# Weight products in two parts: first and second part of a block in turns, instead of eight and eight

## The chip, the cores and the metric

One core of one Trainium2 chip runs the kernel. The metric is the device time of one execution in microseconds (us), as the median of several runs. Engines are named as in the profile: PE is TensorE's matmul, PEld its load of the stationary operand, DVE is VectorE, ACT ScalarE, POOL GpSimd, SP the engine that issues the loads of weights.

## The reference

One layer of a streaming encoder on 256 frames of width 2048, in float32. Two SwiGLU feed-forwards (width 5632) enclose a mixer of two head groups; each part works on an RMS-normalised input and adds to the residual.

```python
x = x + 0.5 * swiglu(rms_norm(x, ffn1_norm), w_gate, w_up, w_down)
p = rms_norm(x, mix_norm) @ w_in          # 2048 x 7456
y = concat(rwkv7_mix(p[..., :RWKV_COLS]), hgrn2_mix(p[..., RWKV_COLS:]))
x = x + y @ w_out
x = x + 0.5 * swiglu(rms_norm(x, ffn2_norm), ...)
return rms_norm(x, final_norm)
```

Nearly all of the arithmetic is in the products with the weights: three matrices of 2048 x 5632 in each feed-forward, `w_in` and `w_out` in the mixer. The mixer's recurrences (a generalised delta rule, and a gated linear recurrence in chunks) are small beside them.

## The kernel before, in words

**Products in parts.** A float32 matrix is split in two: hi is its value rounded to the type fp32r, lo is what is left. A product is hi x hi + hi x lo + lo x hi. With the weight block as the stationary operand (128 x 128), the activations of a slice k are stored as two halves side by side, hi and lo of 256 frames each. So hi of the weights meets 512 columns (both halves of the activations), and lo of the weights meets 256 columns (the first half alone). The function `columns` (L1171) issues the one or the other. Both add to the same accumulator tile `mm` in PSUM: `pt[:, n]` is a bank of 2 x 256 float32, one for each of two blocks n; the two halves of the bank are added when the job ends (`total`, L390).

**Jobs, pieces, units.** The work is a list of jobs (`job`, L387); a job makes 256 output columns from all slices k (16 in most jobs) and has its `consume` function called with the accumulator when the last product is issued. The weights of a job come in pieces of 512 KB: 128 x 1024 numbers, which are kp = 4 slices of 256 columns, so 8 blocks. (One job has kp = 8; two jobs, marked `tok`, have kp = 2 and take the activations as stationary operand and 512 columns of weights as moving one, first with hi of the weights for hi and lo of the activations, then with lo of the weights.) A unit is a slice of a piece with one part: `steps` (L1107) lists the four slices with part 0 and then the four with part 1. So TensorE does eight matmuls of 512 columns and then eight of 256. The first two pieces belong to two jobs and are done slice by slice; there, two matmuls with hi and two with lo follow each other (L1120).

**The main loop** (L1230) goes through the units. After each one it calls `tick` or `poll`: a tick moves the clock by which deferred work and the steps of the background tasks (the recurrences of the mixer, written as generators) are due; `poll` (L308) lets a due task make one step, if a model of the engines says that DVE and ACT are not too far behind. The ticks are counted in shares of a piece, two per piece. So matmuls of the background tasks stand between units in TensorE's queue. Each engine runs its own queue in order; the framework adds semaphores where data or buffers are shared.

**Weights on their way.** SP loads a piece to a `raw` tile (4 buffers, L195). `split` (L1142) then makes its two parts: an ACT cast gives hi, and a subtraction on DVE gives lo; where DVE is behind by the model, `spare` (L395) puts it on POOL. There are 4 buffers for hi and 4 for lo (`wsp`, L196). When the last unit of piece i has been issued, `split_to(i + 5)` (L1153) issues the split of piece i + 4 into the buffers of piece i, and the load of the piece four after that. The cast waits for the last matmul that reads hi of piece i, the subtraction for the cast and for the last one that reads lo.

**The end.** The last two jobs are not in the units: they do all products with lo first and then those with hi in two halves of the frames, so that the final norm of the first half overlaps the second (L1273 on).

Of the kernel before, what the change touches and what calls it, by code (L numbers as in the profile page):

```python
# [18 lines left out]
P = 128  # L19
# [156 lines left out]
def layer_kernel(ctx, tc, a, out):  # L176
# [4 lines left out]
    PE = Products(nc, model)  # L181
# [35 lines left out]
    def ps1():  # L217
        return psp.tile([P, 512], F32, tag="ps", name="ps")
# [89 lines left out]
    def poll():  # L308
        for task in bg[:2]:
            if task[1] <= clock[0] and max(V.until, S.until) <= model.now() + BEHIND:  # L310
                step(task)

    def tick():
        clock[0] += 1
        due = [x for x in later if x[0] <= clock[0]]
        for x in due:
            later.remove(x)
            x[1]()
        poll()


    class Norm:
# [51 lines left out]
        def operand(self, k):  # L374
            return self.parts[k // 2][:, k % 2]
# [729 lines left out]
        return [(jn, w[slab, chunks(chunk, i)], kp * i, kp) for i in range(nk // kp)]  # L1105

    def steps(i):  # L1107
        return [(i, kk, part) for part in range(2) for kk in range(pieces[i][3])]

    pieces, units = [], []  # L1110
    jn = 0
    while jn < len(jobs):
# [4 lines left out]
        else:  # L1117
            pieces += pieces_of(jn)
            jn += 1
    units = [(e, kk, part) for kk in range(4) for e in range(2) for part in range(2)]  # L1120
    for i, x in enumerate(pieces):
        if i >= 2 and x[0] < len(jobs) - 2:
            units += steps(i)
    raws, splits = {}, {}
# [28 lines left out]
    def split_to(n):  # L1153
        while state["split"] < min(n, len(pieces)):
            i = state["split"]
            load_to(i + 4)
            split(i, slice(0, pieces[i][3]))
            del raws[i]
            state["split"] += 1
# [11 lines left out]
    def columns(pt, w, x, n, part, start, stop):  # L1171
        w = w[:, n * P:(n + 1) * P]
        if part == 0:
            PE.matmul(pt.rearrange("p a t -> p (a t)"), w, x.rearrange("p a t -> p (a t)"), start=start, stop=stop)
        else:
            PE.matmul(pt[:, 0, :], w, x[:, 0, :], start=start, stop=stop)
# [50 lines left out]
    defer(15, n1[0].finish)  # L1227
    pts = {}
    ticks = 0
    for i, kk, part in units:  # L1230
        jn, _, k0, kp = pieces[i]
        _, _, _, nk, operand, consume, before, _, tok = jobs[jn]
        k = k0 + kk
        if k == 0 and part == 0:
            if before is not None:
                before()
            pts[jn] = mmp.tile([P, 2, 2, T], F32, tag="mm", name="mm")
        pt = pts[jn]
        x = operand(k)
        w = splits[i][part][:, kk, :]  # L1240
        start, stop = k == 0 and part == 0, k == nk - 1 and part == 1
        if tok:
            for b in range(2):
                o = pt[:, b].rearrange("p a t -> p (a t)")
                for e in range(2 - part):
                    PE.matmul(o, x[:, e, b * P:(b + 1) * P], w, start=start and e == 0, stop=stop)
        else:
            for n in range(1024 // kp // P):
                columns(pt[:, n], w, x, n, part, start, stop)
        if stop:  # L1250
            consume(pt)
            del pts[jn]
        ticks += (4 - 2 * part) / 3 / kp
        if ticks > 0.999:
            ticks -= 1
            tick()
        else:
            poll()
        if kk == kp - 1 and part == 1:
            splits.pop(i)  # L1260
            with tc.high_priority():
                split_to(i + 5)
# [3 lines left out]
    operand, nk = jobs[-1][4], jobs[-1][3]  # L1266
    ws = [[splits[i] for i in sorted(splits) if pieces[i][0] == jn] for jn in (len(jobs) - 2, len(jobs) - 1)]
# [5 lines left out]
    for h in range(2):  # L1273
        pt = mmp.tile([P, 4, T], F32, tag="mm", name="mm")[:, 0:2, :]
        for n in range(2):
            for k in range(nk):
                PE.matmul(pt[:, n, :], weights(2 * h + n, k, 1), operand(k)[:, 0, :],
                          start=k == 0 and n == 0, stop=k == nk - 1 and n == 1)
        x = xT_box[0][:, 12 + 2 * h:14 + 2 * h, :]
# [4 lines left out]
    for b in range(2):  # L1284
        for n in range(4):
            pt = ps1()[:, 0:2 * P].rearrange("p (a t) -> p a t", a=2)
# [62 lines left out]
```

## Time and profile before

| what | value |
|---|---|
| median of 3 runs | 2073.27 us (2073.06 to 2073.94) |
| the profiled execution | 2075.09 us |
| its span, first to last instruction | 2073.3 us |
| granted TensorE clock, mean | 0.994 |
| busy: PE, PEld, DVE, ACT, POOL | 98%, 86%, 67%, 49%, 18% |
| read from HBM | 362.24 MB, 177 GB/s over the span |

The busy time of PE is not its load: matmuls are pipelined, one begins before the end of the one ahead has been modelled, so the start times in the timeline say how fast they follow each other. Nearly all instructions are issued in two helpers (L148 for DVE, ACT and POOL, L168 for TensorE), so groups are told apart by the names of their tiles: `mm<-t,hi` is a product with the first part of the weights, `mm<-t,lo` one with the second.

### The profile page before, as it was taken

How to read it: one execution, taken by the hardware profiler on the slowest of the kernel's cores; microseconds unless marked ns; L12 is line 12 of the kernel's file. 1: busy time of each engine (PE TensorE's matmuls, PEld its weight loads, DVE VectorE, ACT ScalarE, POOL GpSimd, SP SyncE). 2: the span in 40 equal slices, each digit the busy share in tenths (PEclk: the TensorE clock that was granted, in tenths of full speed). 3: DMA queues.
4: the chain of work that ended last, by engine and by line, in shares of the span. 5: the costliest groups of instructions: out<-in, count | busy, mean ns of one | idle time of the engine just before them, and what ended most of it. 6: DMA issues, size and time to landing. Idle time of an engine off the chain costs nothing.

```text
span 2073.3 us, 30664 instructions
## 1 busy us (share of the span) xinstructions
PE 2034.2 (98%) x12286; PEld 1777.3 (86%) x12286; DVE 1384.4 (67%) x1502; ACT 1009.2 (49%) x1185; POOL 367.7 (18%) x218
## 2 busy tenths in 40 slices
PE   8999999999999999899989899999999999999997
PEld 7888888888888888788878788888888888888887
DVE  7655565565566687986898668856555655555557
ACT  6444443444344466455556545544444344434434
POOL 1211110110011122422343114211111011101101
PEclk9999999999999999999999999999999999999999
DMA  7555555555555565443334425555555555555553
GB/s 259 199 189 187 191 186 192 185 191 185 191 188 188 184 230 170 148 140 118 129 113 149 143 96 200 188 188 186 191 192 185 192 186 190 188 188 189 187 192 113
DMA packets 105983, 368.45 MB, mean 178 GB/s; under 512 B 11536, under 2 KB 17808, under 8 KB 105584
## 3 DMA queue, kind: packets, MB, share of 16 engines
q1 hardware_dynamic: 104352, 359.97, 51.9%
q0 software_dynamic: 944, 6.23, 0.8%
q8 instruction: 97, 1.59, 0.3%
q14 instruction: 46, 0.38, 0.1%
q10 hardware_dynamic: 544, 0.28, 0.0%
HBM read 362.24 MB, written 4.19 MB: 177 GB/s over the span
## 4 chain that ended last, share of the span: by engine, by line
PE 90%; DVE 5%; POOL 1%; issue 1%; ACT 1%; DVEq 0%; POOLq 0%; ACTq 0%
PE mm L168 85%; PE ps L168 5%; DVE t L148 3%; DVE lo L148 2%; POOL t L148 1%; ACT t L148 0%; POOL lo L148 0%; DVE xts L148 0%; PE ps L172 0%; DVE b L148 0%; POOL b L148 0%; DVE qk L148 0%; ACT hi L148 0%; ACT q L148 0%; DVEq L1345 0%
## 5 line engine op out<-in xcount | busy, mean ns | idle before, releaser
L168 PE MATMUL mm<-t,hi 128*128 128x512 f32 x5264 | 1329.5, 393 | 3.5 <-DVE t L148 3.1
L148 ACT CAST hi<-raw 128x1024 fp32r<-128x1024 f32 (+1 forms) x685 | 710.9, 1040 | 878.7 <-PE mm L168 764.5
L168 PEld LDWEIGHTS mm<-t,hi 128*128 128x128 f32 x5264 | 946.5, 189 | 174.3 <-ACT hi L148 3.6
L148 DVE TENSOR_TENSOR lo<-raw,hi 128x1024 fp32r<-128x1024 f32 (+1 forms) x613 | 773.5, 1264 | 447.1 <-ACT hi L148 427.6
L168 PEld LDWEIGHTS mm<-t,lo 128*128 128x128 f32 x5296 | 723.4, 190 | 65.8 <-POOL lo L148 7.9
L168 PE MATMUL mm<-t,lo 128*128 128x256 f32 x5296 | 745.1, 283 | 10.3 <-POOL lo L148 6.9
L148 POOL TENSOR_TENSOR lo<-raw,hi 128x1024 fp32r<-128x1024 f32 x72 | 176.1, 2446 | 555.2 <-ACT hi L148 518.0
L148 POOL TENSOR_TENSOR t<-t,inv 128x1024 f32<-128x1024 f32 x22 | 53.0, 2409 | 777.5 <-ACT t L148 777.5
L148 DVE TENSOR_TENSOR t<-t,t 128x512 fp32r<-128x512 f32 (+25 forms) x243 | 169.9, 702 | 11.3 <-ACT t L148 5.3
L148 DVE TENSOR_TENSOR t<-mm,t 128x512 f32<-128x512 f32 x122 | 83.3, 682 | 90.0 <-ACT t L148 89.9
L148 DVE SCALAR_TENSOR_TENSOR xts<-mm,xts 128x512 f32<-128x512 f32 x126 | 86.6, 688 | 76.1 <-PE mm L168 75.7
L148 ACT COPY t<-mm 128x512 f32<-128x512 f32 x122 | 71.0, 582 | 23.9 <-DVE t L148 20.6
L148 ACT CAST t<-t 128x512 fp32r<-128x512 f32 x72 | 44.1, 622 | 28.2 <-DVE t L148 24.8
L148 DVE TENSOR_TENSOR t<-t,inv 128x1024 f32<-128x1024 f32 (+1 forms) x35 | 46.3, 1322 | 1.0
L148 DVE RECIPROCAL t<-t 128x256 f32<-128x256 f32 x24 | 41.5, 1738 | 2.9 <-ACT t L148 2.9
L148 ACT ACTIVATE t<-t 128x1024 f32<-128x1024 f32 (+2 forms) x32 | 32.9, 1028 | 13.8 <-DVE t L148 13.6
L168 PE MATMUL ps<-q,t 128*128 128x128 f32 (+5 forms) x272 | 28.0, 260 | 7.0 <-DVE t L148 6.1
L148 DVE SCALAR_TENSOR_TENSOR t<-xts,vec,t 128x256 fp32r<-128x256 f32 x48 | 25.7, 558 | 13.3 <-ACT t L148 13.3
L168 PEld LDWEIGHTS ps<-q,t 128*128 128x128 f32 (+2 forms) x272 | 26.4, 174 | 9.3 <-issue 6.4
L148 ACT ACTIVATE t<-xts,vec 128x256 fp32r<-128x256 f32 x48 | 23.0, 505 | 22.5 <-DVE xts L148 20.4
L148 DVE SCALAR_TENSOR_TENSOR t<-t,vec,t 128x256 f32<-128x256 f32 x43 | 29.0, 720 | 6.3 <-POOL b L148 4.3
L148 POOL TENSOR_TENSOR t<-t 128x1020 f32<-128x1020 f32 (+1 forms) x7 | 17.8, 2549 | 84.1 <-DVE t L148 78.9
(134 smaller groups left out, 769.0 us busy)
## 6 DMA issues: line engine op xcount, KB each, us to landing
raw<-in_ffn_w_up_dram SPq DMA_DIRECT2D x176, 512.0 KB, 4.2
raw<-in_ffn_w_down_dram SPq DMA_DIRECT2D x176, 512.0 KB, 3.2
raw<-in_ffn_w_gate_dram SPq DMA_DIRECT2D x173, 512.0 KB, 3.4
raw<-in_w_in_dram SPq DMA_DIRECT2D x96, 512.0 KB, 3.2
raw<-in_w_out_dram SPq DMA_DIRECT2D x32, 512.0 KB, 3.2
raw<-in_w_i_dram SPq DMA_DIRECT2D x16, 512.0 KB, 3.3
raw<-in_w_lora_dram SPq DMA_DIRECT2D x6, 512.0 KB, 3.2
spill<-xts POOLq DMA_DIRECT2D x1, 2048.0 KB, 10.1
```

Of the source, the lines that this page charges most:

```text
L148: return fn(*args, **kwargs)
L168: return self.engine.matmul(out, a, b, **kwargs)
```

## The change

For each slice k and each block n the matmul with hi is now followed at once by the one with lo. A unit holds both parts; the loop over parts moves inside the loop over blocks. The first two pieces change in the same way, and in the `tok` jobs the two parts follow each other for each half of the frames. The tick is counted per slice (2 / kp, so after the second and the fourth slice of a piece of four), and `poll` or `tick` is called once for a slice instead of once for a slice and part. `columns`, the splits, the loads, the buffers and the last two jobs stay as they are.

```diff
     def steps(i):
-        return [(i, kk, part) for part in range(2) for kk in range(pieces[i][3])]
+        return [(i, kk, (0, 1)) for kk in range(pieces[i][3])]
...
-    units = [(e, kk, part) for kk in range(4) for e in range(2) for part in range(2)]
+    units = [(e, kk, (0, 1)) for kk in range(4) for e in range(2)]
...
-    for i, kk, part in units:
+    for i, kk, both in units:
...
-        if k == 0 and part == 0:
+        if k == 0:
...
-        w = splits[i][part][:, kk, :]
-        start, stop = k == 0 and part == 0, k == nk - 1 and part == 1
+        ws = [splits[i][part][:, kk, :] for part in both]
         if tok:
             for b in range(2):
                 o = pt[:, b].rearrange("p a t -> p (a t)")
-                for e in range(2 - part):
-                    PE.matmul(o, x[:, e, b * P:(b + 1) * P], w, start=start and e == 0, stop=stop)
+                for part in both:
+                    for e in range(2 - part):
+                        PE.matmul(o, x[:, e, b * P:(b + 1) * P], ws[part], start=k == 0 and part == 0 and e == 0,
+                                  stop=k == nk - 1 and part == 1)
         else:
             for n in range(1024 // kp // P):
-                columns(pt[:, n], w, x, n, part, start, stop)
-        if stop:
+                for part in both:
+                    columns(pt[:, n], ws[part], x, n, part, k == 0 and part == 0, k == nk - 1 and part == 1)
+        if k == nk - 1:
             consume(pt)
             del pts[jn]
-        ticks += (4 - 2 * part) / 3 / kp
+        ticks += 2 / kp
...
-        if kk == kp - 1 and part == 1:
+        if kk == kp - 1:
             splits.pop(i)
```

## Rows read from the trace of the kernel before

**Rows 1.** The page: PE's busy time, granted clock by slices, the chain by line

```profile
PE 2034.2 (98%) x12286; PEld 1777.3 (86%) x12286; DVE 1384.4 (67%) x1502; ACT 1009.2 (49%) x1185; POOL 367.7 (18%) x218
...
PEclk9999999999999999999999999999999999999999
...
PE mm L168 85%; PE ps L168 5%; DVE t L148 3%; DVE lo L148 2%; POOL t L148 1%; ACT t L148 0%; POOL lo L148 0%; DVE xts L148 0%; PE ps L172 0%; DVE b L148 0%; POOL b L148 0%; DVE qk L148 0%; ACT hi L148 0%; ACT q L148 0%; DVEq L1345 0%
```

**Rows 2.** The page's groups: busy us, mean ns of one, idle before, what ended it

```profile
L168 PE MATMUL mm<-t,hi 128*128 128x512 f32 x5264 | 1329.5, 393 | 3.5 <-DVE t L148 3.1
L148 ACT CAST hi<-raw 128x1024 fp32r<-128x1024 f32 (+1 forms) x685 | 710.9, 1040 | 878.7 <-PE mm L168 764.5
...
L168 PE MATMUL mm<-t,lo 128*128 128x256 f32 x5296 | 745.1, 283 | 10.3 <-POOL lo L148 6.9
```

**Rows 3.** Timeline of PE, 700 to 720 us: start us, us, what, count

```profile
702.06 2.00 PE L168 MATMUL mm<-t,hi 128*128 128x512 f32 x8
703.90 1.12 PE L168 MATMUL mm<-t,lo 128*128 128x256 f32 x8
704.85 2.00 PE L168 MATMUL mm<-t,hi 128*128 128x512 f32 x8
...
718.82 1.55 PE L168 MATMUL mm<-t,hi 128*128 128x512 f32 x6
```

**Rows 4.** Timeline of PE in a `tok` job: two pieces, 12 matmuls of 512 columns each

```profile
903.83 1.98 PE L168 MATMUL mm<-hi,t 128*128 128x512 f32 x8
...
906.55 1.98 PE L168 MATMUL mm<-hi,t 128*128 128x512 f32 x8
```

**Rows 5.** Timeline of PE in the last two jobs: 24 matmuls of 256 columns

```profile
2047.08 3.04 PE L168 MATMUL mm<-t,lo 128*128 128x256 f32 x24
2049.95 1.00 PE L168 MATMUL ps<-t,hi 128*128 128x256 f32 x7
```

**Rows 6.** Timeline of PE in the first two pieces: two and two in turns

```profile
8.27 0.63 PE L168 MATMUL mm<-t,hi 128*128 128x512 f32 x2
8.73 0.40 PE L168 MATMUL mm<-t,lo 128*128 128x256 f32 x2
8.97 0.65 PE L168 MATMUL mm<-t,hi 128*128 128x512 f32 x2
...
11.11 0.63 PE L168 MATMUL mm<-t,hi 128*128 128x512 f32 x2
```

**Rows 7.** Timeline of PE in the mixer: a single 512-column product among products with lo

```profile
1250.05 0.51 PE L168 MATMUL mm<-t,lo 128*128 128x256 f32 x3
1250.40 0.40 PE L168 MATMUL ps<-t,bones_r 128*128 128x512 f32 x1
1250.63 0.40 PE L168 MATMUL mm<-t,lo 128*128 128x256 f32 x2
1250.87 0.38 PE L168 MATMUL ps<-t,t 128*128 128x256 f32 x1
```

**Rows 8.** Timeline of ACT and DVE: the split of a piece in the steady stretch

```profile
704.10 1.05 ACT L148 CAST hi<-raw 128x1024 fp32r<-128x1024 f32 x1 [1.74 <-PE mm L168]
...
705.66 1.22 DVE L148 TENSOR_TENSOR lo<-raw,hi 128x1024 fp32r<-128x1024 f32 x1
```

**Rows 9.** PE's waits for lo, 13 to 2040 us: us in total, times, longest

```profile
PE mm L168 <- POOL lo L148: 6.9, 2, 5.8
PE mm L168 <- DVE lo L148: 3.4, 4, 1.6
```

**Rows 10.** Timeline of PE where it waits for lo, in brackets the idle time before

```profile
24.91 1.22 PE L168 MATMUL mm<-t,lo 128*128 128x256 f32 x8 [0.33 <-DVE lo L148]
...
27.97 1.21 PE L168 MATMUL mm<-t,lo 128*128 128x256 f32 x8
...
857.19 1.21 PE L168 MATMUL mm<-t,lo 128*128 128x256 f32 x8 [1.09 <-POOL lo L148]
...
1071.61 2.08 PE L168 MATMUL mm<-t,lo 128*128 128x256 f32 x8 [5.84 <-POOL lo L148]
```

## The prediction

> **What bounds the kernel now.** I read the page first. TensorE is busy 98% of the span, its clock is granted at nine tenths or more in all 40 slices (the 2.4 GHz level), and the chain that ended last lies for 85% of the span on the products into `mm` [rows 1]. These are two groups of nearly equal count: 5264 matmuls of 512 columns with the first part of a weight block (hi) and 5296 of 256 columns with the second (lo); almost nothing was waited for in front of either [rows 2]. So the spacing of these matmuls is the kernel, and the busy times, whose ends are modelled, don't give it. The timeline does: from the start of one run of eight hi to the next is one piece of weights; 702.06 to 718.82 us holds six pieces, 2.793 us each, of which eight hi take 1.84 and eight lo 0.95 [rows 3]. Per pair of one hi and one lo that is 0.3492 us. DVE, ScalarE and the DMA engines are behind TensorE: the ScalarE cast that makes hi waits 764.5 us in all for TensorE to free its buffer [rows 2].
>
> **Part 1: the order of the matmuls.** Counts, columns and operands stay; eight hi and eight lo of a piece become hi, lo, hi, lo. Switches between the two lengths go from two in a piece to sixteen. The trace shows what the lengths cost alone: twelve matmuls of 512 columns in a row (a step with tokens as stationary side) take 906.55 − 903.83 = 2.72 us, 0.2267 each [rows 4]; 24 of 256 columns take 2049.95 − 2047.08 = 2.87 us, 0.1196 each [rows 5]. A pair without any toll for switching would be 0.3463 us, a piece 2.770; the 2.793 of now is 0.023 above it for two switches.
>
> Two places of the trace show shorter turns. At the start of the kernel two hi and two lo take turns: hi at 8.27, lo at 8.73, hi again at 8.97, so 0.70 us for two pairs, 0.350 each [rows 6]. In the mixer single 512-column products of another kind fall among lo: three lo from 1250.05 (0.117 each), one of 512 columns at 1250.40, then lo at 1250.63 and two of them to 1250.87 [rows 7]. The single long one took 0.23 and its neighbours 0.12 each: 0.35 for the pair.
>
> So the toll grows with the length of a run and not with the number of switches: 0.023 for a cycle of eight and eight, 0.70 − 2 × 0.3463 = 0.007 for two and two. I take 0.350 us per pair, from the nearest rows [rows 6, 7]; against 0.3492 that is 0.0008 × 5264 = **+4 us**. The times of a row have two decimals, so a single reading is good to about 0.005 per pair, and the bounds must come from elsewhere. Below: no toll, 0.3463, −0.0029 × 5264 = −15 us. Above: the whole stretch of two and two from 8.27 to its fifth round at 11.11 holds eight pairs in 2.84 us, 0.355 each with some waiting in it [rows 6]: +0.0058 × 5264 = +31 us.
>
> The Trainium skill (TensorE: Matmul & The Clock Gate, section LDWEIGHTS) puts the load of 128 stationary columns at 128 / 1.2 GHz, 107 ns, and its step-by-step section lets the next load run under the running matmul. By that a load fits under 512 columns and just about fills 256; the number of loads under short matmuls stays eight per piece, and the order would not matter beyond the toll: as an estimate, zero. The 0.1196 of the short runs [rows 5], above the load's 107 ns, does not contradict it; no run here shows a load by itself.
>
> Each hi and the lo after it now add into the same accumulator bank back to back, where neighbours alternated between two. That is free: the step with tokens as stationary side already does it at 0.2267 [rows 4], the last products at 0.1196 [rows 5].
>
> **Part 2: lo is needed earlier.** The first lo of a piece runs second instead of ninth, 0.23 us after the start of the piece instead of 1.84. In the steady stretch this is covered: lo is made by DVE some 5 us after the start of the piece four before it (lo from 705.66 to 706.88 [rows 8], in the piece that began at 702.06), and used 4 × 2.793 = 11.2 us after that start; six us remain. Without cover the price is what the late lo blocks: seven hi, 7 × 0.23 = 1.6 us more per episode, since after the wait nearly the whole piece remains where now only eight lo do. Where TensorE waits for lo already, the cover is gone: six waits, 2 for POOL and 4 for DVE, 10.3 us in all [rows 9]. They stand in three stretches: 24.91 and 27.97 at the start, around 857.19, and around 1071.61 in the mixer [rows 10]. Within a stretch the waits share their lateness (lo comes when DVE or POOL gets to it, whatever TensorE did before), so I price each stretch once: 3 × 1.6 = **+5 us**. Bounds: nothing, if the planner's other choices happen to clear them; six waits, 6 × 1.6 = +10 us.
>
> **Part 3: hi is freed later.** The cast of the piece four ahead starts 0.2 us after the eighth hi (703.90 to 704.10 [rows 3, 8]); now hi is in use until the fifteenth matmul of sixteen, seven lo or 0.84 us later. Behind the cast on ScalarE wait copies out of the accumulator and the work of norms and mixer; behind those, DVE. DVE's lo and the free raw buffer move by the same 0.84, and with them the next load, which lands about 3 us after its issue. All of it still ends about five us ahead of use. If that cover were gone it would be 0.84 us per piece; I take zero, and the range holds what it adds in the mixer.
>
> **Part 4: the planner's steps.** A piece still makes two ticks at half and at the end of its TensorE time. Between ticks the mixer's background work is polled four times a piece instead of eight, so a step can start up to 0.35 us later. It is covered by products of weights except where TensorE waits for the mixer; zero, inside the range.
>
> **Sum.** +4 + 5 = +9 us. The profiled execution took 2075.09 us for a span of 2073.3; the three timed runs have a median of 2073.27. Nine us on the median give **2082 us**, 0.4% slower.
>
> **Rivals.**
> *The toll for switching goes.* If it belongs to long runs (for instance because the load under every lo is now the hi's, and the one under every hi has twice the time), a pair takes 0.3463: −15 + 5 = −10, **2063 us**; 2058 if no wait for lo grows either. For it: the toll shrank from 0.023 to 0.007 per cycle between eight and two. Against it: per pair, 0.0028 and 0.0037, it did not shrink at all, and the single long matmul of [rows 7] shows no gain. This ends on the other side of zero.
> *Every switch pays.* If a single hi after a lo is slower than in [rows 7], 0.355 as in the whole start: 31 + 5, **2109 us**; with the full 0.023 of a present cycle on each pair, 0.369, it would be +104, near 2180. Against this stands the 0.70 of [rows 6]. The deciding point is 0.350 per pair: above it the turns cost more than I say.
> *Waits in the mixer take over.* Six us of waiting for POOL in one place [rows 10] show that a planner's bad choice costs as much as my whole sum; a different order of polls can make one or remove one, so **2088 us** with one more of these and 2076 with this one gone. For it: the order of the background steps changes. Against it: one such place in the whole trace.
>
> **How the numbers follow.** A measurement of this kernel tells a change of 0.2%, 4 us, from none. The forecast, pairs at about 0.350 and some us of waits, gets 0.47: its own range is 2070 to 2095, of which 0.32 lies above +4 us, 0.12 within and 0.03 below. The toll going gets 0.28: 0.22 faster and 0.06 eaten up by waits. Every switch paying gets 0.15, all slower. The mixer taking over gets 0.10: 0.05 slower, 0.02 within, 0.03 faster (on the lower rate). Faster 0.28, same 0.20, slower 0.52. The range goes from 2057, the lower rival with few waits, to 2110, the near end of the upper one; about 0.1 lies above it and 0.08 below.
>
> **What would show it.** In the profile after, a steady stretch with turns of single matmuls: six pieces in 16.8 us mean my rate, 16.6 the lower rival, over 17.0 the upper. The count of lo and hi matmuls must be unchanged. Waits of TensorE for lo at the start and in the mixer should be longer by about 1.6 us per stretch, and the cast should start about 0.2 us after the fifteenth matmul of a piece. The prediction is wrong if the steady pair is below 0.348 or above 0.353, or if waits for lo appear outside the three stretches.

## The result, and the profile after

The changed kernel takes 2110.08 us (median of six runs, 2101.41 to 2110.42), the kernel before, run beside it, 2073.93 us (six runs, 2073.06 to 2075.15): 1.0158 times as long, 95% interval 1.0148 to 1.0168. It is 36 us slower, four times the +9 of the forecast and a hair above the range's upper end of 2110. The profiled execution is one of 2110.42 us, with a span of 2108.4 and a mean granted clock of 0.989.

The page of the changed kernel, from its parts on engines, slices and groups:

```profile
PE 2048.5 (97%) x12286; PEld 1778.7 (84%) x12286; DVE 1396.2 (66%) x1505; ACT 1008.7 (48%) x1184; POOL 356.2 (17%) x215
...
PEclk9999999999999999999999898999999999999999
...
L168 PE MATMUL mm<-t,hi 128*128 128x512 f32 x5264 | 1860.9, 398 | 19.2 <-DVE t L148 14.8
L168 PE MATMUL mm<-t,lo 128*128 128x256 f32 x5296 | 1485.1, 281 | 10.6 <-POOL lo L148 8.9
```

Against [rows 1, 2]: the same counts, 12286 matmuls, 5264 and 5296. The wait in front of lo is what it was (10.6 us, 10.3 before). The wait in front of hi went from 3.5 to 19.2 us, and two slices past the middle have a clock below nine tenths. The busy times of the two groups (1860.9 and 1485.1, from 1329.5 and 745.1) say nothing: a matmul that stands alone is credited with its modelled tail, which a run of eight shows once.

To see where the time went I put the two timelines side by side and compared the start of the first matmul with hi of the same piece in both:

| stretch | pieces | change in us |
|---|---|---|
| start | to 8 | +0.8 |
| first feed-forward | 8 to 256 | −4.8 |
| its end and the start of the mixer | 256 to 272 | +4.1 |
| mixer | 272 to 400 | +22.2 |
| end of the mixer, start of the second feed-forward | 400 to 424 | +6.5 |
| second feed-forward and the last two jobs | 424 to the end | +8.3 |

The sum is 37.1 at the start of the last matmul; 2.0 less lie behind it in this execution, which leaves the 35.1 by which the span grew. Two things stand out. The feed-forwards, which do the same work, changed in opposite directions, and some 29 us lie around the mixer, where I had counted about 2.

**Two spacings.** The timeline of PE, first at 700 us, then at 1600 us (the columns as in [rows 3]):

```profile
699.62 0.39 PE L168 MATMUL mm<-t,hi 128*128 128x512 f32 x1
699.85 0.28 PE L168 MATMUL mm<-t,lo 128*128 128x256 f32 x1
...
705.86 0.39 PE L168 MATMUL mm<-t,hi 128*128 128x512 f32 x1
...
1600.04 0.40 PE L168 MATMUL mm<-t,hi 128*128 128x512 f32 x1
...
1600.39 0.40 PE L168 MATMUL mm<-t,hi 128*128 128x512 f32 x1
...
1600.76 0.40 PE L168 MATMUL mm<-t,hi 128*128 128x512 f32 x1
...
1601.10 0.40 PE L168 MATMUL mm<-t,hi 128*128 128x512 f32 x1
...
1606.40 0.40 PE L168 MATMUL mm<-t,hi 128*128 128x512 f32 x1
```

Each stretch holds 18 pairs, from 699.62 to 705.86 and from 1600.04 to 1606.40: 6.24 us, 0.3467 a pair, in the first feed-forward, and 6.36 us, 0.3533, in the second. Before it was 0.3492 in both feed-forwards, as in [rows 3]. In the second the pairs go in threes: from 1600.04 on they take 0.35, 0.37 and 0.34 us, and the same again behind that; those of the first are even. A stretch that has one of the two spacings keeps it, for hundreds of us, until TensorE next has to wait or other matmuls come between. I call them quick and slow. Over 248 and some 240 pieces of eight pairs they make the −4.8 and most of the +8.3 of the table.

**Waits.** PE's waits over the whole run (us in total, times, longest), the changed kernel:

```profile
PE ps L168 <- DVE t L148: 17.6, 6, 10.9
PE mm L168 <- DVE t L148: 14.8, 5, 10.4
PE mm L168 <- POOL lo L148: 8.9, 2, 5.5
PE mm L168 <- DVE xts L148: 4.2, 4, 1.9
PE mm L168 <- DVE lo L148: 1.6, 1, 1.6
```

and the kernel before:

```profile
PE ps L168 <- DVE t L148: 11.1, 6, 5.4
...
PE mm L168 <- DVE t L148: 3.1, 3, 1.2
```

All lines of this view add to 52.9 us after and 30.4 before. Two waits of over 10 us, both for the mixer's own work on DVE, carry most of the 22.5 between them. The timeline of the changed kernel around both, all engines, in brackets the idle time before:

```profile
1169.94 1.40 PE L168 MATMUL ps<-q,t 128*128 128x128 f32 x5 [10.89 <-DVE t L148]
...
1295.23 3.31 DVE L148 TENSOR_TENSOR t<-t,t 128x1024 f32<-128x1024 f32 x1
...
1300.04 2.34 POOL L148 TENSOR_TENSOR t<-t,t 128x1024 f32<-128x1024 f32 x1 [2.58 <-DVE t L148]
1302.41 1.28 DVE L148 TENSOR_TENSOR t<-t,ps 128x512 f32<-128x512 f32 x2 [2.45 <-POOL t L148]
1303.13 1.22 ACT L148 CAST t<-t 128x512 fp32r<-128x512 f32 x2 [8.09 <-DVE t L148]
1304.52 0.80 PE L168 MATMUL mm<-t,hi 128*128 128x512 f32 x1 [10.44 <-DVE t L148]
...
1305.33 0.63 PE L168 MATMUL mm<-t,hi 128*128 128x512 f32 x1
...
1305.97 0.63 PE L168 MATMUL mm<-t,hi 128*128 128x512 f32 x1
```

The second wait is new. At 1294.08 TensorE has done the products with the first half of the recurrences' output and needs the second half, which is still being normalised: DVE, POOL, DVE, ACT one after the other, until 1304.5. POOL's step of this chain begins 6 us after TensorE ran out of work. In the kernel before it is this line of POOL's timeline, 9 us ahead of the first product with the second half (1282.24), so nothing waits:

```profile
1272.94 2.39 POOL L148 TENSOR_TENSOR t<-t,t 128x1024 f32<-128x1024 f32 x1 [5.32 <-DVE t L148]
```

Behind the wait the matmuls start at the 1.2 GHz level: a pair from 1305.33 to 1305.97 takes 0.64 us, not 0.35. So a wait costs more than its length. It shows in one window of both kernels (us, busy us of PE, PEld, DVE, ACT, POOL, granted clock, DMA share, GB/s), first before, then after; the changed kernel is 12 to 29 us behind there, so the two do not hold quite the same pieces:

```profile
1250.00:1350.00 100.00, 100.00 (x571) 88.02 (x571) 83.93 (x89) 56.28 (x70) 34.47 (x14) 1.00 0.54 184
1250.00:1350.00 100.00, 84.29 (x499) 70.85 (x498) 74.45 (x77) 42.11 (x57) 31.27 (x13) 0.93 0.39 137
```

PE was never idle in it before and is idle for 15.7 us after, and the granted clock drops from 1.00 to 0.93. Of the 37.1 us, 22.5 are idle time and 3.5 the two spacings. Most of the 11 left over is the lower clock: in all stretches with a granted clock of 0.50 together, PE is busy for 11.2 us before and for 25.4 us after. About half of the 14.2 more is lost, by the 0.64 and 0.35 of a pair; that is an estimate of 7 us. The rest, about 4 us, I put down to the turns' spacing inside the mixer, which is not shown.

### The profile page after: what moved, and what is told of

Same layout as the page of the kernel before. It is cut to its first block, busy times and chain, and to the rows that moved or that the text cites. A ratio compares the mean times of both kernels' runs of the same rounds, so it can differ in the third digit from the quotient of the medians.

```text
span 2108.4 us, 30658 instructions
## 1 busy us (share of the span) xinstructions
PE 2048.5 (97%) x12286; PEld 1778.7 (84%) x12286; DVE 1396.2 (66%) x1505; ACT 1008.7 (48%) x1184; POOL 356.2 (17%) x215
## 5 line engine op out<-in xcount | busy, mean ns | idle before, releaser
L168 PE MATMUL mm<-t,hi 128*128 128x512 f32 x5264 | 1860.9, 398 | 19.2 <-DVE t L148 14.8
L168 PE MATMUL mm<-t,lo 128*128 128x256 f32 x5296 | 1485.1, 281 | 10.6 <-POOL lo L148 8.9
L168 PEld LDWEIGHTS mm<-t,hi 128*128 128x128 f32 x5264 | 991.7, 188 | 256.2 <-DVE t L148 13.7
L148 DVE TENSOR_TENSOR lo<-raw,hi 128x1024 fp32r<-128x1024 f32 (+1 forms) x616 | 782.0, 1271 | 505.2 <-ACT hi L148 504.7
L168 PEld LDWEIGHTS mm<-t,lo 128*128 128x128 f32 x5296 | 1003.2, 190 | 13.1 <-POOL lo L148 9.6
L148 POOL TENSOR_TENSOR lo<-raw,hi 128x1024 fp32r<-128x1024 f32 x69 | 170.9, 2477 | 562.0 <-ACT hi L148 529.6
L168 PE MATMUL ps<-q,t 128*128 128x128 f32 (+5 forms) x272 | 28.5, 266 | 13.5 <-DVE t L148 12.1
L168 PE MATMUL mm<-hi,t 128*128 128x512 f32 x128 | 40.2, 395 | 0.0
L148 ACT COPY t<-ps 32x512 f32<-32x512 f32 (+8 forms) x44 | 19.7, 447 | 37.3 <-PE ps L168 36.5
## 6 DMA issues: line engine op xcount, KB each, us to landing
spill<-xts POOLq DMA_DIRECT2D x1, 2048.0 KB, 10.4
```

Of the source, the lines that this page charges most:

```text
L148: return fn(*args, **kwargs)
L168: return self.engine.matmul(out, a, b, **kwargs)
```

## Experiments

The kernel before ran beside every group: 2074.82 us beside the first four (twelve runs), 2075.15 beside the next four (fourteen), 2075.58 and 2074.84 beside the last two groups (seven each). None of these kernels leaves out a part of the computation.

### Is it the polls? Eight polls a piece with turns, and four without

In the changed kernel the background of the mixer is offered a step four times a piece, not eight. One run gives the changed kernel its polls back:

```diff
                 for part in both:
                     columns(...)
+                if n == 0:
+                    poll()
...
```

(The `tok` jobs get the same poll after the first half of the frames.)

> The changed kernel with a poll of the background tasks after the first block of a slice too, so eight polls a piece as before the change; matmuls in turns as in the changed kernel. Between piece 272 and piece 400 (the mixer) the changed kernel lost 22 us to the one before, most of it in two waits of 10.9 and 10.4 us for the recurrences. Theory (polls): these come from the recurrences being polled half as often; they go, and the time is 2084 to 2092 us. Rival (late lo and hi): the mixer loses because the second part is needed earlier and the first is freed later; the time stays at 2104 to 2112 us.

Measured: 2091.0 us (2087.43 to 2092.76), ratio 1.0072 (1.0057 to 1.0087). It is 16 us above before, where the changed kernel is 36. The mixer (pieces 272 to 400) now adds about 9 us in place of 22, and the wait ahead of the second half of the output projection is gone.

The other takes half of the polls from the kernel before:

```diff
-        else:
+        elif kk == 1:
             poll()
```

> The kernel before, eight and eight, but with four polls and ticks a piece instead of eight; nothing else. Theory (polls): the mixer loses some 22 us without any change of the matmuls' order, 2088 to 2102 us, with waits of TensorE for the recurrences of about 10 us each; the feed-forwards are as before to within 1 us. Rival (late lo and hi): 2070 to 2078 us.

Measured: 2083.95 us (2082.48 to 2085.39), ratio 1.0041 (1.0026 to 1.0056): +9, less than I had expected of it. But the wait that belongs to few polls is there again. The timeline of PE in this run:

```profile
1288.70 3.78 PE L168 MATMUL mm<-t,hi 128*128 128x512 f32 x8 [4.57 <-DVE t L148]
1292.28 1.91 PE L168 MATMUL mm<-t,lo 128*128 128x256 f32 x8
```

Again it stands ahead of the second half of the output projection, and again the matmuls behind it run at the lower level: eight hi take 3.58 us, where [rows 3] have 1.84.

### Where does it lie? Turns in one part of the kernel alone

Turns in the feed-forwards' jobs only, the mixer's jobs as before:

```diff
+    mix0 = len(jobs)
     mixer(to_ffn2)
+    mix1 = len(jobs)
...
     def steps(i):
+        if mix0 <= pieces[i][0] < mix1:
+            return [(i, kk, (part,)) for part in range(2) for kk in range(pieces[i][3])]
...
```

> Turns in the two feed-forwards alone; the jobs of the mixer go eight and eight with eight polls a piece. The mixer should be as in the kernel before. What is left: start +1, first feed-forward -5 by its spacing, its end +4 (TensorE waits for DVE to empty the accumulator), second feed-forward +8 if its matmuls fall into the slow spacing of 0.3533 us a pair, -5 if into the quick one of 0.3467. Theory (the spacing is one of two, set where a stretch begins): about 2082 us or about 2069 us, and the spacing within a feed-forward is one of these two numbers and no other. Rival (the spacing belongs to the place: quick in the first, slow in the second): always 2082 us.

Measured: 2081.0 us (median of nine, 2079.72 to 2094.82), ratio 1.004 (1.0025 to 1.0055): +6. The first feed-forward is quick and the second slow, as in the changed kernel, so this run does not tell the theory from the rival. The run of 2094.82 us has no profile; it lies above the median by about what a slow first feed-forward would add (248 pieces of 0.053 us, 13 us), and its granted clock, 0.995, is no lower than that of the others.

Turns and their four polls in the mixer's jobs only (the condition above with `not`):

> The counterpart of the run with turns in the feed-forwards alone: turns with four polls a piece in the jobs of the mixer, eight and eight with eight polls in the feed-forwards. Theory (the mixer holds most of the loss, by its background steps, and the parts add): 2074 + 27 = 2101 us, 2095 to 2106, with the wait ahead of the second half of the output projection of about 10 us. Rival (the mixer loses because it is entered at another time and state from the feed-forward): 2070 to 2085 us.

Measured: 2102.25 us (2098.15 to 2103.72), ratio 1.0125 (1.0108 to 1.0142): +27, and not a tenth of a us of it in the steady stretches of the feed-forwards. Its waits of PE:

```profile
PE ps L168 <- DVE t L148: 17.6, 6, 10.9
PE mm L168 <- DVE t L148: 15.3, 5, 10.4
```

The longest, 10.9 and 10.4, are those of the changed kernel to the tenth. And 27 and 6 make 33 of the 36. So the two parts are nearly independent, and three quarters of the loss are the mixer's.

The fourth corner, turns in the mixer with eight polls (the poll after the first block put into the run above, for units that hold both parts):

> Turns in the mixer's jobs alone, as in the run with turns there, but with a poll after the first block of each slice, so eight polls a piece as before. The theory that the turns are nearly harmless in the mixer and that their 27 us come with the halved polls: the two waits of over 10 us at the head of the second half of the output projection and ahead of the products of the attention go, about +9 us remain as in the kernel that had turns everywhere and eight polls, so 2083 to 2087 us, ratio 1.004 to 1.006. The rival that the turns themselves put the mixer out of step, whatever the polls: 2096 us or more, with at least one of the two waits still near 10 us. A halved poll that costs the same with and without turns (9 us) would give 27 - 9 = +18, 2093 us.

Measured: 2086.46 us (2085.15 to 2089.91), ratio 1.0059 (1.0042 to 1.0076). Its waits:

```profile
PE ps L168 <- DVE t L148: 9.9, 4, 6.9
PE mm L168 <- DVE lo L148: 9.1, 4, 3.6
...
PE mm L168 <- DVE t L148: 1.7, 2, 1.1
```

The 10.4 us are gone, the 10.9 have become 6.9; in their place DVE's lo is late, up to 3.6 us. All waits add up to 31.6 us, only 1.2 more than before; where the rest of the +12 lies is shown further down. That gives a square of four: eight polls and the old order 0, four polls and the old order +9, eight polls and turns +12, four polls and turns +27. Halving the polls costs 9 us without the turns and 15 with them; the turns cost 12 with eight polls and 18 with four. Neither is harmless by itself, and together they cost 6 us more than their sum. The theory had the size of the run right, but it had called the turns nearly harmless, and 12 us are not that.

### Does an earlier need for lo do it? And do more polls help?

The old order with a piece's eight lo ahead of its eight hi:

```diff
     def steps(i):
-        return [(i, kk, part) for part in range(2) for kk in range(pieces[i][3])]
+        kp, first = pieces[i][3], not pieces[i][2]
+        return ([(i, 0, 0)] if first else []) + [(i, kk, 1) for kk in range(kp)] + [(i, kk, 0) for kk in range(first, kp)]
...
```

> The kernel before, eight and eight with eight polls, but with the eight lo of a piece ahead of the eight hi (the first slice of a job still begins with hi). So lo is needed at the start of a piece and hi freed at its end, as in the changed kernel, without single turns and without fewer polls. Theory (late hi at the ends of the stages): spacing 0.349 in both feed-forwards; the end of the first feed-forward loses 2 to 4 us and the end of the mixer 3 to 7, the start 1 to 2: 2079 to 2088 us. Rival (these losses belong to the turns or the polls): 2071 to 2077 us.

Measured: 2087.0 us (2084.58 to 2089.01), ratio 1.0059 (1.0042 to 1.0075): +12, of it about 6 in the mixer, 3 at its end, and one or so each at the start and at the end of the first feed-forward. That is inside the theory's range, but half of it lies in the mixer, where the theory had put nothing. PE waits 12.4 us for POOL's lo (6.9 before), 6.8 at the longest. So an order that needs lo early does cost in the mixer, but the two waits of the changed kernel are not in this run.

Sixteen polls a piece in the kernel before:

```diff
             for n in range(1024 // kp // P):
                 columns(pt[:, n], w, x, n, part, start, stop)
+                if n == 0:
+                    poll()
```

> The kernel before, eight and eight, with a poll after the first block of a unit too: sixteen polls a piece instead of eight. Theory (fewer polls are late polls, so more of them do no harm): 2066 to 2076 us. Rival (the mixer's order was fitted to its eight polls, and any other number spoils it): 2079 to 2090 us, as with four polls.

Measured: 2087.51 us (2086.26 to 2088.69), ratio 1.006 (1.0045 to 1.0075): +12. My theory in its plain form (few polls make steps late, more do no harm) falls here. No wait ahead of the second half of the output projection, but another one, and behind it again eight hi at the lower level (3.75 us, 2.00 in [rows 3]); the timeline of PE:

```profile
1087.69 3.75 PE L168 MATMUL mm<-t,hi 128*128 128x512 f32 x8 [9.34 <-DVE t L148]
```

Four different edits that move what the mixer is offered by fractions of a us (half the polls, twice the polls, lo first, turns with eight polls) each cost 9 to 12 us. Waits are only a part of that. The table has all waits of PE, and how long PE is busy in the stretches with a granted clock of 0.50, each from the profiled execution:

| kernel | median against before, us | PE's waits, us | PE busy at 0.50, us |
|---|---|---|---|
| before | 0 | 30.4 | 11.2 |
| four polls, old order | +9 | 32.8 | 22.8 |
| sixteen polls, old order | +12 | 37.7 | 20.3 |
| lo first | +12 | 36.0 | 17.0 |
| turns in the mixer, eight polls | +12 | 31.6 | 26.2 |
| turns in the mixer, four polls | +27 | 51.3 | 23.0 |
| the changed kernel | +36 | 52.9 | 25.4 |

Take half of what the last column has above its first row as time lost. Then added waits and clock together come within 4 us of each difference up to the +27. In the run with four polls in the old order, and in that with turns in the mixer and eight polls, the lower clock costs more than the added waits. One such stretch of the latter run, where PE had waited 1.98 us at 862.54 (columns as in the windows above):

```profile
863.94:870.76 6.82, 6.52 (x31) 5.43 (x31) 6.68 (x9) 0.58 (x1) 0.00 (x0) 0.50 0.68 244
```

What is special to few polls is one wait, that for the recurrences ahead of the output projection: 10.4 us, 10.4 and 4.6 in the three runs with four polls, none in those with eight or sixteen.

### What sets the two spacings?

In the profile after, stretches that begin with a hi after a wait for the accumulator are mostly slow, and those that begin with a lo mostly quick. So I suspected the first matmuls of a stretch. The run with turns in the feed-forwards only, with each feed-forward job's first slice as hi, hi, lo, lo, and turns from there:

```diff
+            if k == 0 and len(both) == 2:
+                for part in both:
+                    for n in range(2):
+                        columns(...)
...
```

> As the run with turns in the feed-forwards alone (2081.0 us), but the first slice of every job there goes hi, hi, lo, lo; after it hi, lo in turns. So the turns are broken once in every job, in both feed-forwards in the same way. Theory (the spacing of a stretch is set by what came ahead of it and kept till the next break): both feed-forwards show the same spacing in their steady parts, either 0.3467 us a pair (about 2068 us) or 0.3533 (about 2090 us). Rival (the spacing belongs to the place): quick in the first, slow in the second as before, 2079 to 2085 us.

Measured: 2080.86 us (2079.53 to 2084.9), ratio 1.003 (1.0019 to 1.004). The jobs do not share a spacing, they alternate. The timeline of PE in two neighbouring jobs:

```profile
103.06 0.40 PE L168 MATMUL mm<-t,hi 128*128 128x512 f32 x1
...
104.83 0.40 PE L168 MATMUL mm<-t,hi 128*128 128x512 f32 x1
...
115.05 0.40 PE L168 MATMUL mm<-t,hi 128*128 128x512 f32 x1
...
117.13 0.40 PE L168 MATMUL mm<-t,hi 128*128 128x512 f32 x1
```

Five pairs in 1.77 us, 0.354, and six in 2.08, 0.347; so it goes on through both feed-forwards, and the mean, 0.350, is about that of before. The same beginning turns slow to quick and quick to slow. That the beginning gives the spacing is refuted in my wording, and so is the rival that the place in the kernel does, since both feed-forwards do the same. What is left: a break in the turns can flip the spacing, and what stood ahead counts.

Next, in place of a change of order, something foreign ahead of the turns: two products of 128 x 1 numbers, in float32, of a tile of zeros into a scratch tile that nothing reads, written once ahead of piece 448. The profile shows each as two matmuls.

```diff
+        if i == 448 and kk == 0:
+            kick = ps1()
+            for b in range(2):
+                PE.matmul(kick[:, b:b + 1], sts[0][:, 0, :], ones[:, 0:1], start=True, stop=True)
```

> As the run with turns in the feed-forwards alone, with two tiny float32 products (128 x 1, zeros) ahead of piece 448, once, in the second feed-forward after its last wait. In the changed kernel's trace such products stood ahead of two stretches (764.7 and 886.5 us), and both were quick. Theory (set by what came ahead): from there to the end the second feed-forward is quick, 0.3467 instead of 0.3533 a pair over 226 pieces of 8 pairs, 12 us less: 2066 to 2071 us. Rival (the place): 2079 to 2085 us, and nothing changes at piece 448.

Measured: 2068.44 us (median of six, 2067.9 to 2080.62), ratio 0.9979 (0.9961 to 0.9998), 12.6 below the same kernel without them. In the profiled execution they ran earlier than written, at 1343.77: nothing holds them, and they fell where, without them, a load of TensorE waits 0.43 us for DVE. Behind them the stretch is quick, to the end; without them it turns slow at that place and stays so. One of the six runs took 2080.62, about the time of a slow first feed-forward more, at a granted clock of 0.995, no lower than the others'; that run has no profile.

Then the test that takes the mixer out of it: turns only in the steady pieces of both feed-forwards (16 to 239, and 448 to the end), the rest as before, with the tiny products ahead of each stretch and without:

```diff
     def steps(i):
+        if not (16 <= i < 240 or i >= 448):
+            return [(i, kk, (part,)) for part in range(2) for kk in range(pieces[i][3])]
...
+        if i in (16, 448) and kk == 0 and 0 in both:
+            kick = ps1()
+            for b in range(2):
+                PE.matmul(kick[:, b:b + 1], sts[0][:, 0, :], ones[:, 0:1], start=True, stop=True)
```

> Turns only where nothing waits: pieces 16 to 239 and 448 to the end, each begun with the two tiny products; all else eight and eight with eight polls, so start, ends of stages and mixer as in the kernel before. Theory: each piece in turns saves 0.0200 us (2.7933 - 8 x 0.3467), 224 + 226 pieces, 9 us: 2064 to 2067 us, faster than both kernels. Rival (the place): the first stretch saves 4.5 us, the second loses 7.5: 2076 to 2079 us.

Measured: 2066.03 us (2065.52 to 2069.04), ratio 0.9961 (0.9947 to 0.9975). It beats both kernels, by 9 and by 44 us. The same kernel without the second hunk:

> The run with steady turns (2066.0 us) without its two pairs of tiny products, so that the turns at pieces 16 and 448 begin straight behind eight lo. Theory (what stands ahead sets the spacing): in the run with turns in the feed-forwards alone the turns that began behind eight lo at 1320 us were slow; both stretches become slow, 0.3533 a pair, 450 pieces x 0.053 = 24 us more, about 2090 us; one of them slow, 2078 us. Rival (the tiny products do nothing and steady stretches are quick once nothing waits in them): 2064 to 2068 us.

Measured: 2089.04 us (2087.88 to 2091.12), ratio 1.0066 (1.0051 to 1.0081). The timelines of PE, with the products:

```profile
55.77 0.88 PE L168 MATMUL mm<-t,lo 128*128 128x256 f32 x6
56.49 0.50 PE L168 MATMUL ps<-cst,st 128*128 128x1 f32 x4
56.85 0.47 PE L168 MATMUL mm<-t,hi 128*128 128x512 f32 x1
...
400.14 0.39 PE L168 MATMUL mm<-t,hi 128*128 128x512 f32 x1
...
406.38 0.39 PE L168 MATMUL mm<-t,hi 128*128 128x512 f32 x1
```

and without:

```profile
400.04 0.40 PE L168 MATMUL mm<-t,hi 128*128 128x512 f32 x1
...
406.40 0.40 PE L168 MATMUL mm<-t,hi 128*128 128x512 f32 x1
```

Again 18 pairs each: 0.3467 with them, 0.3533 without, for the whole of both stretches. 450 pieces at 2.793 − 8 × 0.3467 = 0.020 us less make the 9 us; the other way it is 450 × 0.033 = 15 us, where 13.5 are measured. That what stands ahead of the turns decides which of the two spacings they take is shown; turns right behind eight lo are slow, turns behind the tiny products quick. What in TensorE holds the state is open. The trace does not tell the two apart but by the start times: in both a load begins with the matmul ahead of it.

## Why the prediction was right or wrong

The direction was right, slower at a chance of 0.52; the size was not. Step by step:

**What bounds the kernel.** Held. TensorE remains the bound, the counts are unchanged, and the steady stretches end on its spacing alone.

**Part 1, the rate.** The forecast took one rate for the whole kernel, 0.350, and +4 us. There are two, 0.3467 and 0.3533, so that both marks I had set for being wrong were met, below 0.348 and above 0.353. The first is the rival in which the toll goes (0.3463), the second close to the one in which every switch pays (0.355); I had set them against each other as alternatives, and the kernel does both. The net of both feed-forwards was −4.8 + 8.3 = +3.5, and the +4 agrees with it by chance only. The step that failed is reading a rate out of 0.70 us for two pairs [rows 6] or one single product [rows 7]: rows that short can't show that a rate has two values. The Trainium skill (TensorE: Matmul & The Clock Gate, section LDWEIGHTS) gives a load one duration by its columns, 107 ns for 128; from that no two spacings of one and the same sequence would follow, and the measurement decides.

**Part 2, lo needed earlier.** The forecast was 1.6 us in each of three stretches, +5. Of [rows 10] the line at 27.97 shows no wait: of the six waits of before one lies at the start, two around 850, three around 1070. The timeline of PE after, in the same three stretches, in the second and third at other pieces than before:

```profile
24.61 0.39 PE L168 MATMUL mm<-t,lo 128*128 128x256 f32 x1 [1.62 <-DVE lo L148]
...
840.57 0.58 PE L168 MATMUL mm<-t,lo 128*128 128x256 f32 x1 [3.42 <-POOL lo L148]
...
1083.06 0.58 PE L168 MATMUL mm<-t,lo 128*128 128x256 f32 x1 [5.52 <-POOL lo L148]
```

Each is now the only wait for lo of its stretch. The start has 1.3 us more, nearly as priced, though only 0.8 of it is left eight pieces into the kernel; the second stretch has 1.8 more, the third 2.9 less, so that the sum of waits for lo is 10.5 us against 10.3. The stretches were right, the sum of +5 isn't found in the waits for lo. With turns everywhere and eight polls it is: 12.4 us for DVE's lo and 2.8 for POOL's, 4.9 more than before. With turns and eight polls in the mixer alone the sum is 10.9. How late lo is depends on what else DVE and POOL have been given.

**Part 3, hi freed later: zero.** In the steady stretches it is zero, and the cast starts 0.2 us behind the fifteenth matmul of a piece, as forecast. At the end of the first feed-forward something is lost: the accumulator comes free late there. The timeline after:

```profile
742.82 2.39 POOL L148 TENSOR_TENSOR lo<-raw,hi 128x1024 fp32r<-128x1024 f32 x1 [2.92 <-ACT hi L148]
742.85 3.44 DVE L148 TENSOR_TENSOR lo<-raw,hi 128x1024 fp32r<-128x1024 f32 x1
...
746.55 1.41 DVE L148 SCALAR_TENSOR_TENSOR xts<-mm,xts 128x512 f32<-128x512 f32 x2
...
748.10 0.56 PE L168 MATMUL mm<-t,hi 128*128 128x512 f32 x1 [1.93 <-DVE xts L148]
```

TensorE waits 1.93 us for DVE to empty its accumulator, and DVE had a lo ahead of that in its queue, which took 3.44 us and not the 1.22 of [rows 8]. The kernel before has no wait there. The prediction said that copies out of the accumulator wait behind the cast, and then priced it at nothing. But the later hi alone does not make this wait. The run with turns in the feed-forwards and the tiny products (2068.44 us) does the same as the changed kernel up to there, and its lines at this place are:

```profile
741.46 1.22 DVE L148 TENSOR_TENSOR lo<-raw,hi 128x1024 fp32r<-128x1024 f32 x1
741.91 3.03 POOL L148 TENSOR_TENSOR lo<-raw,hi 128x1024 fp32r<-128x1024 f32 x1 [3.13 <-ACT hi L148]
```

Here DVE begins ahead of POOL, its lo takes 1.22 us, and TensorE waits 0.3. In the changed kernel POOL begins its lo 0.03 us ahead of DVE, and DVE's ends 1.08 us after POOL's. Of the 616 lo that DVE makes in that trace, the 547 with no POOL instruction beside them take at most 1.23 us, and 38 of the other 69 take longer. So what is lost here hangs on which of two subtractions begins first: pieces 256 to 272 add 4.1 us in the changed kernel, 0.4 in the run with the tiny products, and 0.3 with turns everywhere and eight polls.

**Part 4, half the polls: zero.** This is the step that failed most. The prediction wrote that a later step is covered "except where TensorE waits for the mixer", and then put zero for just that place. It is the place that mattered: turns and polls together cost 27 us there in a run by themselves. The polls alone cost 9, the turns alone 12, so the prediction's silence on what the turns do inside the mixer (Part 3 left it to the range) failed as well. The lateness of one step (up to 0.35 us) was the wrong unit: POOL's step ahead of the second half came some 15 us later against TensorE's work than before, and waits changed by 5 to 10 us. I explain that by the planner, which issues another step next when a poll moves; no run here holds the steps' order fixed while the polls move, so this link is argued and not shown. And behind a wait TensorE runs at the 1.2 GHz level, some 7 us of the 36, which I had not counted.

**The rivals.** The mixer taking over got 0.10 and one more wait of six us, with "one such place in the whole trace" against it. It was the main mechanism: one wait twice as long, another new and of 10 us, where I had priced one of six. The evidence I set against it was thin: that a wait is rare before says little when the order of the steps around it is about to change.

Two of the six runs of the changed kernel lie below the others (2101.41 and 2104.4) and have no profile of their own. Their granted clock is 0.991 and 0.990, that of the others 0.988 and 0.989, so they spent less time at the lower level; 0.002 of the span is 4 us. A second feed-forward that is quick throughout would be 13 us less, more than either step. What differs stays open.

## What to carry to other kernels

Where a queue of background steps is fed from inside a main loop, count how often it is fed before and after the change, and price each wait of the bound engine on that work at its full length and the slow matmuls behind it, not at the delay of one step. Read a steady rate from a steady stretch, and where none exists before the change, keep both readings as cases that can hold side by side. And put a reordering only where the rest doesn't hang on the order: turns in the steady feed-forwards, with a defined start, gained 9 us, while turns in the mixer cost 12 us with the old number of polls and 27 with half of them.

## What was not expected of the hardware

One and the same endless sequence of matmuls, 512 and 256 columns in turns, ran at 0.3467 or at 0.3533 us a pair at a granted clock of 1.00, and kept its value for almost 700 us. Four matmuls of one column ahead of it, 0.36 us in all, made it quick in both steady stretches; the old order of eight and eight, 0.3492, lies between the two.

Behind the long waits TensorE ran at its 1.2 GHz level: pairs of 0.64 us behind 10.44 us of idle time, eight hi in 3.58 us behind 4.57. The matmuls there take up to twice as long. Short waits can cost so too: behind 1.93 us of idle time at 748.10 the granted clock of the changed kernel is 0.50 (748.34 to 751.75), behind 2.04 us at 864.97 it stays at 1.00.

DVE's subtraction for lo took 1.22 us by itself and up to 3.44 us with a subtraction on POOL beside it.
